# A decoder layer on one core: the first feed-forward product as seven block products (Strassen) in place of eight

## The chip, the core and the metric

The kernel runs on one core of a Trainium2 chip. The metric is the device time of one execution in microseconds; the median of three runs is compared. PE is TensorE (matmuls), DVE is VectorE, ACT is ScalarE, POOL is GpSimd, and SP is the engine whose queue issues all DMAs.

## The reference, cut to what matters

One layer over 512 tokens of width 1024, in float32. The front (norm, a wide input projection, and three token mixers: a state-space scan, differential attention and RWKV-7), the merge of their branches and the output projection stay as they are. What the change works on is the last line but one:

```python
x = x + (merged @ w_out[i]).astype(x.dtype)
h2 = rms_norm(x, norm2_g[i])
gu = h2 @ w_ffn_in[i]                         # 512 x 1024 times 1024 x 5632
x = x + ((silu(gu[..., :D_FF]) * gu[..., D_FF:]) @ w_ffn_out[i]).astype(x.dtype)   # D_FF = 2816
```

## The kernel before

Everything is kept transposed: a tile is 128 channels by the 512 tokens. A dense product (class `Dense`, `__call__`) makes 128 output columns at a time in one PSUM bank and runs over blocks of 128 input channels. To keep float32 precision with float32r matmuls, both factors are split into a high part (a float32r cast, on ACT) and a low part (the remainder, on DVE), and every block takes three matmuls of 512 columns: high x high (L1264), high weights x low activations (L1265), low weights x high activations (L1266). Activations are split once; weights are split as they come: `Dense.load` moves 128x512 values (four blocks, 256 KB) from DRAM (L1201, on SP), casts them (ACT, L1202) and takes the low part (DVE, L1203). Three raw tiles and five each of the high and low parts rotate, and a cast waits until PE is done with the tile that it overwrites.

The code is written in program order; a scheduler decides the order in which each engine gets its instructions, and each engine then works in that order. The stages around the change are these:

- The output projection (`take_res`, eight tiles d): the PSUM result is added to x (DVE, L1475), the sum x2 is multiplied by the norm's gain and split into `act_hi` and `act_lo` (L229, L230), and its squares are added up (`Rms.add`: ACT, L1287; POOL, L1292).
- The first feed-forward product, 22 blocks f: a gate product and an up product, 8 blocks of channels with 3 matmuls each, so 48 matmuls of 512 columns. On the gate's result: times R, the inverse norm (DVE, L1495), tanh (ACT, L1496), L1497 (DVE), and times R again (POOL, L1498, the only instruction that POOL has in a block). Then the product with the up half (DVE, L1501), and the split (L229, L230).
- The second feed-forward product, eight tiles d over 22 blocks (`take_out`): the result is added to x2, which has stayed in SBUF (L1506), and goes out.

## Time and profile before

| | us |
|---|---|
| runs | 1045.37, 1044.82, 1041.97; median 1044.82 |
| profiled execution | 1045.61, its span 1043.8 |
| PE busy | 1007.8 |
| DVE busy | 660.6 |
| ACT busy | 406.1 |
| POOL busy | 136.8 |

The profile records each instruction's start and duration, and what the engine waited for. Matmuls are pipelined: their records overlap, so the distance between starts tells what one costs. On DVE, too, the next instruction starts some 0.08 us before the record of the last one ends. The first feed-forward product runs from about 666 to 917 us of the span.

### The profile page before, as it was taken

How to read it: one execution, taken by the hardware profiler on the slowest of the kernel's cores; microseconds unless marked ns; L12 is line 12 of the kernel's file. 1: busy time of each engine (PE TensorE's matmuls, PEld its weight loads, DVE VectorE, ACT ScalarE, POOL GpSimd, SP SyncE). 2: the span in 40 equal slices, each digit the busy share in tenths (PEclk: the TensorE clock that was granted, in tenths of full speed). 3: DMA queues.
4: the chain of work that ended last, by engine and by line, in shares of the span. 5: the costliest groups of instructions: out<-in, count | busy, mean ns of one | idle time of the engine just before them, and what ended most of it. 6: DMA issues, size and time to landing. Idle time of an engine off the chain costs nothing.

```text
span 1043.8 us, 15814 instructions
## 1 busy us (share of the span) xinstructions
PE 1007.8 (97%) x5664; PEld 808.9 (77%) x5664; DVE 660.6 (63%) x1696; ACT 406.1 (39%) x799; POOL 136.8 (13%) x161
## 2 busy tenths in 40 slices
PE   6999999989899999999999999999999999999998
...
PEclk8999999999999999999999999999999999999999
...
GB/s 233 112 81 99 84 127 52 71 53 42 133 68 77 102 72 131 112 141 92 152 225 261 189 163 99 84 91 94 98 92 91 96 96 91 92 100 110 108 115 41
DMA packets 96798, 114.08 MB, mean 109 GB/s; under 512 B 44400, under 2 KB 46192, under 8 KB 96720
## 3 DMA queue, kind: packets, MB, share of 16 engines
...
q14 instruction: 34, 0.28, 0.1%
...
## 4 chain that ended last, share of the span: by engine, by line
PE 80%; DVE 13%; DMA 3%; issue 2%; ACT 1%; POOL 0%; SPq 0%; DVEq 0%; ACTq 0%; POOLq 0%
PE bank L1265 21%; PE bank L1266 21%; PE bank L1264 21%; DVE wl_s L1203 2%; PE bank L441 1%; PE bank L603 1%; PE bank L1161 1%; PE bank L608 1%; PE bank L1250 1%; PE bank L452 1%; PE bank L1249 1%; PE bank L1248 1%; DMA ar<-ymix 1%; PE bank L235 1%; PE bank L611 1%
## 5 line engine op out<-in xcount | busy, mean ns | idle before, releaser
L1202 ACT CAST wh_s<-wr_s 128x512 fp32r<-128x512 f32 (+1 forms) x286 | 175.1, 614 | 359.8 <-PE bank L1265 323.4
L1264 PE MATMUL bank<-act_hi,wh_s 128*128 128x512 f32 x712 | 288.3, 405 | 6.8 <-ACT wh_s L1202 5.9
L1203 DVE TENSOR_TENSOR wl_s<-wr_s,wh_s 128x512 fp32r<-128x512 f32 (+1 forms) x286 | 200.5, 702 | 144.9 <-ACT wh_s L1202 144.1
L1265 PE MATMUL bank<-act_lo,wh_s 128*128 128x512 f32 x712 | 288.9, 406 | 2.1 <-DVE act_lo L230 2.1
L1266 PE MATMUL bank<-act_hi,wl_s 128*128 128x512 f32 x712 | 288.5, 405 | 0.0
L1264 PEld LDWEIGHTS bank<-act_hi,wh_s 128*128 128x128 f32 x712 | 135.5, 190 | 37.6 <-ACT wh_s L1202 6.1
L1265 PEld LDWEIGHTS bank<-act_lo,wh_s 128*128 128x128 f32 x712 | 135.6, 190 | 33.7 <-DVE act_lo L230 4.3
L1266 PEld LDWEIGHTS bank<-act_hi,wl_s 128*128 128x128 f32 x712 | 135.6, 190 | 29.9 <-issue 0.7
L1265 PE MATMUL bank<-act,wh_s 128*128 128x512 f32 x176 | 69.8, 396 | 0.0
L1264 PE MATMUL bank<-act,wh_s 128*128 128x512 f32 x176 | 69.8, 396 | 0.0
L1266 PE MATMUL bank<-act,wl_s 128*128 128x512 f32 x176 | 69.8, 396 | 0.0
L1265 PE MATMUL bank<-bl,wh_s 128*128 128x512 f32 x112 | 44.7, 399 | 1.4 <-DVE bl L227 1.1
L1264 PE MATMUL bank<-bh,wh_s 128*128 128x512 f32 x112 | 44.6, 398 | 1.0 <-ACT bh L229 0.6
L1266 PE MATMUL bank<-bh,wl_s 128*128 128x512 f32 x112 | 44.4, 396 | 0.0
L1264 PEld LDWEIGHTS bank<-act,wh_s 128*128 128x128 f32 x176 | 33.1, 188 | 8.1
L1266 PEld LDWEIGHTS bank<-act,wl_s 128*128 128x128 f32 x176 | 33.1, 188 | 8.1
L1265 PEld LDWEIGHTS bank<-act,wh_s 128*128 128x128 f32 x176 | 33.1, 188 | 8.1
L1462 POOL TENSOR_TENSOR ar<-ar,ar 128x512 f32<-128x512 f32 x10 | 16.0, 1598 | 176.3 <-DVE ar L1460 176.3
L1498 POOL TENSOR_TENSOR ar<-ar,ar 128x512 f32<-128x512 f32 x15 | 19.8, 1322 | 146.5 <-DVE ar L1497 146.5
L1501 DVE TENSOR_TENSOR ar<-ar,bank 128x512 f32<-128x512 f32 x22 | 15.1, 688 | 37.1 <-PE bank L1266 37.1
L1495 DVE TENSOR_TENSOR ar<-bank,ar 128x512 f32<-128x512 f32 x22 | 15.2, 692 | 36.0 <-PE bank L1266 34.8
L1250 PE MATMUL bank<-wl_s,act_hi 128*128 128x256 f32 x128 | 37.1, 290 | 0.0
...
## 6 DMA issues: line engine op xcount, KB each, us to landing
wr_s<-in_w_in SPq DMA_DIRECT2D x88, 256.0 KB, 2.8
wr_s<-in_w_ffn_in SPq DMA_DIRECT2D x88, 256.0 KB, 2.6
wr_s<-in_w_ffn_out SPq DMA_DIRECT2D x40, 256.0 KB, 2.7
gate<-ar SPq DMA_DIRECT2D x24, 256.0 KB, 2.7
wr_s<-in_w_branch SPq DMA_DIRECT2D x24, 256.0 KB, 3.0
ar<-gate SPq DMA_DIRECT2D x24, 256.0 KB, 3.3
ar<-in_xT SPq DMA_DIRECT2D x16, 256.0 KB, 3.5
wr_s<-in_w_kv SPq DMA_DIRECT2D x16, 256.0 KB, 3.4
```

Source lines behind the costliest of these rows:

```text
L235: self.nc.tensor.matmul(ps[:, b, :], sq[:, b * P:(b + 1) * P], self.c("sel"), start=True, stop=True)
L441: nc.tensor.matmul(pa[:, c * P:(c + 1) * P], kb[rows, 4 * q + c].rearrange("p a t -> p (a t)"), ar[rows, 4 * q + c].rearrange("p a t -> p ...
L1202: nc.scalar.copy(wh, raw)
L1203: nc.vector.tensor_tensor(wl, raw, wh.bitcast(F32), ALU.subtract)
L1250: nc.tensor.matmul(ps, xh, wl[:, j], start=False, stop=k == nk - 1)
L1264: nc.tensor.matmul(ps, wh[:, j], hi(k), start=k == 0, stop=False)
L1265: nc.tensor.matmul(ps, wh[:, j], lo(k), start=False, stop=False)
L1266: nc.tensor.matmul(ps, wl[:, j], hi(k), start=False, stop=k == nk - 1)
L1462: nc.gpsimd.tensor_tensor(g, g, acc, ALU.add)
L1495: nc.vector.tensor_tensor(w, ps, R, ALU.mult)
L1498: nc.gpsimd.tensor_tensor(t, t, R, ALU.mult)
L1501: dense(A["w_ffn_in"][2 * f + 1], KD, h_hi, h_lo, lambda ps: nc.vector.tensor_tensor(t, t, ps, ALU.mult))
```

## The change

The first feed-forward product of a block f is taken as a product of 2x2 blocks: tokens 0 to 255 and 256 to 511, input channels 0 to 511 and 512 to 1023, and the gate and up columns. Strassen's method in Winograd's form makes it from seven products in place of eight, each over 4 blocks of channels, 3 matmuls of 256 columns each: 84 matmuls of 256 columns per block f.

- Activations: `Winograd.take` replaces the split in `take_res`. For d below 4 it makes h, and the difference t1 of its two token halves; for d from 4 on also t2 and t3, three half tiles. All are split into high and low parts; what `act_hi` and `act_lo` hold for d below 4 in the second half of the tokens is t1.
- Weights: `Winograd.pair` loads four raw tiles (a00 and a01 of the gate columns, a10 and a11 of the up columns), now in a ring of six, and makes the sums s1 to s4 on POOL (L1356). Seven tiles are split in place of four: a00, s1, s2, a01, s3, s4, a11.
- Results: products add up in PSUM, and ACT copies a bank's half after four of them (L1381, L1385, L1389, L1395). L1401 and L1403 add copies and PSUM, L1405, L1406 (tanh), L1407 and L1409 (POOL) are the old steps, L1410 (POOL) adds two copies, L1412 and L1413 are the product with the up half, and the split ends the block.
- x2 is written to DRAM in `take_res` and read back in `take_out`, all on SP. Pools that the mixers needed (among them small tiles and constants) are closed after the merge, and their memory is used again; the eight PSUM banks are dealt out anew.

```diff
@@ Env
+    def leave_mixers(self):
+        assert not self.scopes
+        self.mctx.close()
+        self.spool = self.later.enter_context(self.tc.tile_pool(name="fpool", bufs=1, reuse_waits="tile"))
+        self.phase = "f"
+        free = [b for n in ("pd", "prw", "ps") for b in self.pools[n].free]
+        assert len(free) == 8
+        for n, k in (("pf", 4), ("pd", 2), ("ps", 2)):
+            self.pools[n] = Slots(n, [free.pop(0) for _ in range(k)])
...
@@ Dense.load: the raw, high and low weight tiles
-            return E.small(tag, [P, KB * P], dt, bufs=n)[:, 0:w.shape[1] * ncol].rearrange("p (k n) -> p k n", n=ncol)
+            return self.ring(tag, dt, n)[:, 0:w.shape[1] * ncol].rearrange("p (k n) -> p k n", n=ncol)
...
+    def ring(self, tag, dt, n):
+        tiles, at = self.rings.setdefault(tag, ([], [0]))
+        if len(tiles) < n:
+            tiles.append((self.E.spool if self.E.phase else self.E.cpool).tile([P, KB * P], dt, name=self.E.uid(tag)))
+        t = tiles[at[0] % n]
+        at[0] += 1
+        return t
...
+class Winograd:
+    H, N = 4, 256
+    def __init__(self, E, dense, act_hi, act_lo):
+        self.E, self.dense, self.act = E, dense, (act_hi, act_lo)
+        self.t = [E.spool.tile([P, 3, self.H, self.N], F32R, name=f"wg_t{i}") for i in range(2)]
+        self.h = E.arena("wg_h", F32, (P, self.H, T))
+        self.t1 = E.arena("wg_t1", F32, (P, 2 * self.H, self.N))
+        self.banks = E.pools["pf"], E.pools["pd"]
+    def take(self, d, x, gain):
+        E, nc, N = self.E, self.E.nc, self.N
+        V, j = nc.vector, d % self.H
+        hi, lo = self.act
+        a, b = slice(0, N), slice(N, 2 * N)
+        with E.scope("s"):
+            h = self.h[:, d] if d < self.H else E.slot("wg_hd")
+            nc.scalar.activation(h, x, AF.Copy, scale=gain)
+            t1 = self.t1[:, j]
+            if d < self.H:
+                E.split(h[:, a], hi[:, d, a], lo[:, d, a])
+                V.tensor_tensor(t1, h[:, b], h[:, a], ALU.subtract)
+                E.split(t1, hi[:, d, b], lo[:, d, b])
+                return
+            E.split(h, hi[:, d], lo[:, d])
+            t2, t3 = self.t1[:, self.H + j], E.slot("wg_t3")
+            V.tensor_tensor(t2, h[:, b], t1, ALU.subtract)
+            V.tensor_tensor(t3[:, a], h[:, b], self.h[:, j, b], ALU.subtract)
+            V.tensor_tensor(t3[:, b], h[:, a], t2, ALU.subtract)
+            for i, t in enumerate((t2, t3[:, a], t3[:, b])):
+                E.split(t, self.t[0][:, i, j], self.t[1][:, i, j])
+    def pair(self, wg, wu, R, ah, al):
+        E, nc, d = self.E, self.E.nc, self.dense
+        V, G, N, H = nc.vector, nc.gpsimd, self.N, self.H
+        blocks = {}
+        def raw(i, k):
+            t = d.ring("wr", F32, WF)
+            nc.sync.dma_start(t.rearrange("p (k n) -> p k n", n=P), d.blocks((wg, wu)[i], KD, P)[k])
+            return t
+        def add(x, y, op):
+            t = E.slot("wg_s")
+            G.tensor_tensor(t, x, y, op)
+            return t
+        def product(bank, w, b, start):
+            hi, lo = d.ring("wh", F32R, WB[1]), d.ring("wl", F32R, WB[1])
+            E.split(w, hi, lo)
+            ps = bank[:, 0:N]
+            for j in range(H):
+                c = slice(j * P, (j + 1) * P)
+                for n, (x, y) in enumerate(((hi, 0), (hi, 1), (lo, 0))):
+                    nc.tensor.matmul(ps, x[:, c], b(y, j), start=start and j == n == 0, stop=j == H - 1 and n == 2,
+                                     skip_group_check=True)
+        def act(k, t):
+            return lambda y, j: self.act[y][:, H * k + j, t * N:(t + 1) * N]
+        def tee(i):
+            return lambda y, j: self.t[y][:, i, j]
+        x, v = (E._take("pf", (P, 512), False) for _ in range(2))
+        y = E._take("pd", (P, 512), False)
+        keep = E.slot("wg_c", (P, 2, N))
+        keep2 = E.slot("wg_c2", (P, 2, N))
+        a00 = raw(0, 0)
+        product(x, a00, act(0, 0), True)
+        nc.scalar.copy(keep[:, 0], x[:, 0:N])
+        a10, a11 = raw(1, 0), raw(1, 1)
+        s1 = add(a10, a11, ALU.add)
+        product(y, s1, act(0, 1), True)
+        nc.scalar.copy(keep2[:, 1], y[:, 0:N])
+        s2 = add(s1, a00, ALU.subtract)
+        E.free(s1)
+        product(x, s2, tee(0), False)
+        nc.scalar.copy(keep[:, 1], x[:, 0:N])
+        a01 = raw(0, 1)
+        product(v, a01, act(1, 0), True)
+        s3 = add(a00, a10, ALU.subtract)
+        product(x, s3, tee(1), False)
+        E.free(s3)
+        nc.scalar.copy(keep2[:, 0], x[:, 0:N])
+        s4 = add(a01, s2, ALU.subtract)
+        E.free(s2)
+        product(y, s4, act(1, 1), False)
+        E.free(s4)
+        w, t = E.slot("fw"), E.slot("ft")
+        V.tensor_tensor(w[:, 0:N], keep[:, 0], v[:, 0:N], ALU.add)
+        E.free(v)
+        V.tensor_tensor(w[:, N:], keep[:, 1], y[:, 0:N], ALU.add)
+        E.free(y, keep)
+        V.tensor_tensor(w, w, R, ALU.mult)
+        nc.scalar.activation(t, w, AF.Tanh, scale=0.5)
+        V.scalar_tensor_tensor(t, t, 1.0, w, ALU.add, ALU.mult)
+        E.free(w)
+        G.tensor_tensor(t, t, R, ALU.mult)
+        G.tensor_tensor(keep2[:, 1], keep2[:, 0], keep2[:, 1], ALU.add)
+        product(x, a11, tee(2), False)
+        V.tensor_tensor(t[:, N:], t[:, N:], keep2[:, 1], ALU.mult)
+        V.tensor_tensor(t[:, 0:N], t[:, 0:N], x[:, 0:N], ALU.mult)
+        E.free(x, keep2)
+        E.split(t, ah, al, 0.5)
...
@@ trunk_kernel
+    E.leave_mixers()
...
+    win = Winograd(E, dense, act_hi, act_lo)
+    x2dr = [E.dram("x2", [P, T]) for _ in range(KD)]
     def take_res(d):
         def f(ps):
             nc.vector.tensor_tensor(x2[d], x2[d], ps, ALU.add)
-            E.split(x2[d], h_hi(d), h_lo(d), E.pc("n2", d))
+            win.take(d, x2[d], E.pc("n2", d))
             norm.add(x2[d])
+            nc.sync.dma_start(x2dr[d], x2[d])
+            E.free(x2[d])
         return f
...
-            t = E.slot("ft")
-
-            def take_g(ps):
-                w = E.slot("fw")
-                nc.vector.tensor_tensor(w, ps, R, ALU.mult)
-                nc.scalar.activation(t, w, AF.Tanh, scale=0.5)
-                nc.vector.scalar_tensor_tensor(t, t, 1.0, w, ALU.add, ALU.mult)
-                nc.gpsimd.tensor_tensor(t, t, R, ALU.mult)
-
-            dense(A["w_ffn_in"][2 * f], KD, h_hi, h_lo, take_g)
-            dense(A["w_ffn_in"][2 * f + 1], KD, h_hi, h_lo, lambda ps: nc.vector.tensor_tensor(t, t, ps, ALU.mult))
-            E.split(t, ah[f], al[f], 0.5)
+            win.pair(A["w_ffn_in"][2 * f], A["w_ffn_in"][2 * f + 1], R, ah[f], al[f])
     def take_out(d):
         def f(ps):
-            nc.vector.tensor_tensor(x2[d], x2[d], ps, ALU.add)
-            nc.sync.dma_start(outT[d * P:(d + 1) * P], x2[d])
+            with E.scope("s"):
+                x = E.slot("xo")
+                nc.sync.dma_start(x, x2dr[d])
+                nc.vector.tensor_tensor(x, x, ps, ALU.add)
+                nc.sync.dma_start(outT[d * P:(d + 1) * P], x)
```

On DVE, in the middle of the first feed-forward product of the kernel before, one block f reads so (`wl` is the low part of weights, `act` the split result):

```order
L1495 TENSOR_TENSOR ar_13_78<-bank_80,ar_12_77 128x512
L1203 TENSOR_TENSOR wl_s_141<-wr_s_132,wh_s_140 128x512
L1497 SCALAR_TENSOR_TENSOR ar_13_78<-ar_13_78 128x512
L1203 TENSOR_TENSOR wl_s_146<-wr_s_99,wh_s_145 128x512
L1501 TENSOR_TENSOR ar_13_78<-ar_13_78,bank_81 128x512
L1203 TENSOR_TENSOR wl_s_101<-wr_s_111,wh_s_100 128x512
L230 SCALAR_TENSOR_TENSOR act_5964<-ar_13_78,act_5964 128x512
L1203 TENSOR_TENSOR wl_s_113<-wr_s_132,wh_s_112 128x512
```

The same place on DVE in the changed kernel (L244 is the low part, of weights or of sums; L247 that of the result), up to the low part of the block's result; two more L244 follow before the next L1401:

```order
L1401 TENSOR_TENSOR ar_14_82<-ar_13_81,bank_83 128x256
L244 TENSOR_TENSOR wl_144<-ar_13_81,wh_143 128x512
L244 TENSOR_TENSOR wl_149<-ar_14_82,wh_148 128x512
L1403 TENSOR_TENSOR ar_14_82<-ar_13_81,bank_86 128x256
L1405 TENSOR_TENSOR ar_14_82<-ar_14_82,ar_12_80 128x512
L244 TENSOR_TENSOR wl_104<-wr_6080,wh_103 128x512
L1407 SCALAR_TENSOR_TENSOR ar_12_80<-ar_12_80,ar_14_82 128x512
L244 TENSOR_TENSOR wl_116<-ar_12_80,wh_115 128x512
L1412 TENSOR_TENSOR ar_12_80<-ar_12_80,ar_14_82 128x256
L1413 TENSOR_TENSOR ar_12_80<-ar_12_80,bank_84 128x256
L244 TENSOR_TENSOR wl_140<-ar_13_81,wh_137 128x512
L247 SCALAR_TENSOR_TENSOR act_6053<-ar_12_80,act_6053 128x512
```

Eight instructions per block have become fourteen, and the low parts of the next block's weights stand between the steps of this block's result.

On POOL, the end of the output projection and the start of the first feed-forward product in the kernel before:

```order
L1292 TENSOR_TENSOR ar_13_78<-ar_13_78,ar_12_77 128x512 x2
L1292 TENSOR_TENSOR ar_13_78<-ar_13_78 128x512
L1292 TENSOR_TENSOR ar_13_78<-ar_13_78,ar_12_77 128x512
L1498 TENSOR_TENSOR ar_13_78<-ar_13_78,ar_12_77 128x512 x2
L1498 TENSOR_TENSOR ar_12_77<-ar_12_77 128x512
```

POOL in the middle of that product in the changed kernel, between two L1409 (`wr` are raw weights: a00 in 6082, a10 in 102, a11 in 114, a01 in 135; so s3, s1, s2, s4 in this order):

```order
L1409 TENSOR_TENSOR ar_12_80<-ar_12_80 128x512
L1356 TENSOR_TENSOR ar_12_80<-wr_6082,wr_102 128x512
L1356 TENSOR_TENSOR ar_12_80<-wr_102,wr_114 128x512
L1356 TENSOR_TENSOR ar_13_81<-ar_12_80,wr_6082 128x512
L1356 TENSOR_TENSOR ar_14_82<-wr_135,ar_13_81 128x512
L1410 TENSOR_TENSOR ar_13_81<-ar_13_81 128x256
L1409 TENSOR_TENSOR ar_13_81<-ar_13_81,ar_12_80 128x512
```

One instruction per block has become six: the four sums for the next block, then L1410 and L1409 of this one.

## Rows read from the trace of the kernel before

**Rows 1.** Page: busy time per engine; tenths busy per slice; chain that ended last.

```profile
PE 1007.8 (97%) x5664; PEld 808.9 (77%) x5664; DVE 660.6 (63%) x1696; ACT 406.1 (39%) x799; POOL 136.8 (13%) x161
...
PE   6999999989899999999999999999999999999998
...
PEclk8999999999999999999999999999999999999999
...
PE 80%; DVE 13%; DMA 3%; issue 2%; ACT 1%; POOL 0%; SPq 0%; DVEq 0%; ACTq 0%; POOLq 0%
```

**Rows 2.** Busy us by stretch: length, PE, PEld, DVE, ACT, POOL, clock, DMA.

```profile
750.00:800.00 50.00, 50.00 (x215) 40.21 (x214) 23.71 (x36) 16.89 (x27) 5.17 (x4) 1.00 0.31 95
```

**Rows 3.** Timeline, POOL, first feed-forward product: start, duration, instruction [idle before, releaser].

```profile
699.37 1.30 POOL L1498 TENSOR_TENSOR ar<-ar 128x512 f32<-128x512 f32 x1 [9.83 <-DVE ar L1497]
...
913.03 1.29 POOL L1498 TENSOR_TENSOR ar<-ar,ar 128x512 f32<-128x512 f32 x1 [9.94 <-DVE ar L1497]
```

**Rows 4.** Timeline, PE, a key and value product: first and last of 34 matmuls.

```profile
317.09 0.28 PE L1248 MATMUL bank<-wh_s,act_hi 128*128 128x256 f32 x1
...
321.04 0.28 PE L1248 MATMUL bank<-wh_s,act_hi 128*128 128x256 f32 x1
```

**Rows 5.** Groups by line and shape: count, busy us, mean ns, idle before.

```profile
L1202 ACT CAST wh_s<-wr_s 128x512 fp32r<-128x512 f32 x278 | 171.9, 620 | 354.3 <-PE bank L1265 317.9 <-issue 15.3 <-DMA wr_s<-in_w_in 6.1
...
L229 ACT ACTIVATE act<-ar 128x512 fp32r<-128x512 f32 x22 | 13.9, 633 | 7.9 <-DVE ar L1501 7.9
...
L1089 ACT ACTIVATE ar<-bank 128x256 f32<-128x256 f32 x8 | 3.1, 384 | 5.9 <-PE bank L1250 4.4 <-DVE ar L1152 1.5
...
L1203 DVE TENSOR_TENSOR wl_s<-wr_s,wh_s 128x512 fp32r<-128x512 f32 x278 | 197.1, 710 | 142.7 <-ACT wh_s L1202 141.8 <-issue 0.2
...
L1203 DVE TENSOR_TENSOR wl_s<-wr_s,wh_s 128x256 fp32r<-128x256 f32 x8 | 3.4, 424 | 2.2 <-ACT wh_s L1202 2.2
```

**Rows 6.** POOL's L1498 and L1462 (ns min/median/max); timeline around one L1462.

```profile
L1498 POOL TENSOR_TENSOR ar<-ar,ar x15: 1286/1296/1707, 678.1 to 913.0; 128x512 f32<-128x512 f32 x15
...
L1462 POOL TENSOR_TENSOR ar<-ar,ar x10: 1298/1608/1675, 558.9 to 621.9; 128x512 f32<-128x512 f32 x10
...
579.51 0.68 DVE L1203 TENSOR_TENSOR wl_s<-wr_s,wh_s 128x512 fp32r<-128x512 f32 x1
579.77 1.58 POOL L1462 TENSOR_TENSOR ar<-ar 128x512 f32<-128x512 f32 x1 [1.23 <-DVE ar L1460]
```

**Rows 7.** POOL's L916 (ns); timeline of DVE and POOL around the longest.

```profile
L916 POOL TENSOR_TENSOR ar<-s_pr,ar x4: 1493/1592/4812, 102.4 to 263.6; 128x512 f32<-128x512 f32 x4
...
263.56 4.81 POOL L916 TENSOR_TENSOR ar<-s_pr,ar 128x512 f32<-128x512 f32 x1 [6.27 <-PE bank L978]
...
264.68 0.67 DVE L683 TENSOR_TENSOR ar<-s_rr,ar 128x512 f32<-128x512 f32 x1
...
265.28 0.15 DVE L219 SCALAR_TENSOR_TENSOR rqy_rw<-rqt_rw,rqi_rw 128x8 f32<-128x8 f32 x1
...
267.32 1.08 DVE L219 SCALAR_TENSOR_TENSOR rqy_rw<-rqt_rw,rqy_rw 128x8 f32<-128x8 f32 x1
```

**Rows 8.** Timeline, DVE and POOL around another sum of POOL.

```profile
218.08 0.18 DVE L685 TENSOR_TENSOR ar<-ar,ar 128x8 f32<-128x8 f32 x1
...
222.94 1.29 POOL L918 TENSOR_TENSOR ar<-ar,ar 128x512 f32<-128x512 f32 x1
222.99 1.26 DVE L685 TENSOR_TENSOR ar<-ar,ar 128x16 f32<-128x16 f32 x1
```

**Rows 9.** Timeline, DVE and POOL: an instruction of DVE that reads PSUM.

```profile
271.36 0.67 DVE L307 TENSOR_TENSOR ar<-bank,R 128x512 f32<-128x512 f32 x1
271.37 1.09 POOL L917 TENSOR_TENSOR ar<-s_pi,ar 128x512 f32<-128x512 f32 x1
```

**Rows 10.** Page, DMA issues: count, KB each, median us from issue to landing.

```profile
wr_s<-in_w_ffn_in SPq DMA_DIRECT2D x88, 256.0 KB, 2.6
...
ymix<-ar SPq DMA_DIRECT2D x12, 256.0 KB, 2.2
```

65 lines of the change are left out of this document (36 added, 29 removed).

## The prediction

> **What bounds the kernel now.** The page comes first: PE, the engine of the matmuls, is busy for 97% of the span, and 80% of the chain that ended last is PE's, most of it in the three matmul lines of the dense product [rows 1]. The next view is the table by stretches. The change works in the first feed-forward product, from about 666 to 917 us, and in a stretch from its middle PE is busy for all of 50 us at full clock, while DVE (VectorE) is busy for 24, ACT (ScalarE) for 17 and POOL (GpSimd) for 5 [rows 2]. So PE alone sets the time there, and the change starts from there. Its unit is one block f of 22: 128 gate and 128 up columns. POOL has exactly one instruction per block, L1498, so its start times give the period. From the first to the last of the 20 that one answer lists there are 19 periods: (913.03 - 699.37)/19 = 11.245 us [rows 3]. A block has 2 x 8 x 3 = 48 matmuls of 512 columns, so one costs 0.234 us. The durations in the rows (0.39 us) overlap; the spacing of starts is the price.
>
> **PE's part.** A block becomes 7 x 4 x 3 = 84 matmuls of 256 columns. The trace has such matmuls in the key and value products: 34 in a row start from 317.09 to 321.04 us, so 33 steps of 0.120 us [rows 4], barely more than half of 0.234. PE's need falls from 11.25 to 84 x 0.1197 = 10.05 us per block, by 1.19 us, or 26 us over 22 blocks. That is all that the arithmetic can give, and only if everything else fits into 10.05 us.
>
> **What the other engines get, each alone** [rows 5]. ACT now has seven casts of 0.62 us, four copies of 256 columns out of PSUM (the nearest row, L1089, has 0.385), the tanh and the split at 0.63: 7.15 us. DVE has ten instructions of 512 columns (seven low parts, the product with R at L1405, L1407 and the low part of the result) and four of 256 (L1401 to L1413 are lines of the changed kernel, as in the orders shown with the change). The low part's row says 0.71 us, but back to back the next one starts after 0.60 us, as 264.68 to 265.28 shows [rows 7]; the 256-wide low part is 0.28 us shorter (0.424 against about 0.70), so 0.32. DVE's sum is 10 x 0.60 + 4 x 0.32 = 7.3 us. POOL had one instruction per block and gets six: four sums of weights, L1409, and L1410 at half width. Undisturbed, one of 512 columns takes 1.295 us; I take 0.65 for the half: 7.1 us. Each alone would fit. The question is whether they run side by side.
>
> **DVE and POOL do not.** In the stage before, L1462, a POOL sum with the same operands, has a median of 1.608 us against 1.296 for L1498 [rows 6]. Its timeline tells why. DVE's L1203 starts at 579.51 and would let the next go after 0.60 us, at 580.11; the POOL instruction starts at 579.77 and ends at 581.35, that is 1.24 us after DVE lets go, so it did next to nothing during the 0.34 us of overlap [rows 6]. The extreme is another sum [rows 7]: L916 (median of its four 1.592 us) takes 4.81 us while DVE runs instructions end to end, many with two SBUF inputs as at 264.68, and at 267.32 an instruction of 128x8 that otherwise takes 0.15 us holds DVE for 1.08 us, while POOL at last works. It goes the other way round as well [rows 8]: a 128x16 DVE instruction that starts at 222.99, just behind a POOL sum, takes 1.26 us. About 0.18 of that is its own (the row of 128x8 on the same line), so POOL kept it out for 1.08 us; with the 0.05 us between the starts a POOL sum occupies what they share for 1.13 us. An instruction with one input in PSUM is not held: L307 takes 0.67 us beside L917 [rows 9].
>
> The Trainium skill has this as a rule, in "SBUF — State Buffer", section "SBUF: two separate sides": one port pair serves GpSimd and the VectorE instructions that have two SBUF inputs or run in a two-port mode, it is locked for a whole instruction, and the other engine waits. The trace agrees, except that POOL's hold is shorter than its record (1.13 of 1.295 us). By the rule, with every record held whole, a block would take 14.5 us and the kernel 1119, the time of rival (b) below; by the holds that the rows show it takes 13.0.
>
> **The sum for a block.** Of DVE's fourteen instructions eleven have two SBUF inputs: ten of 0.60 and L1412, of 0.32 us: 6.3. L1401, L1403 and L1413 read PSUM and are free. POOL: 5 x 1.13, and for the half width between 0.4 and 0.65, so 0.55: 6.2. Together 12.5 us that can't overlap, against 10.05 on PE. To this come gaps: DVE finishes L1405, ACT does the tanh (0.63 us), DVE can fill it with one low part of 0.60, then L1407, then POOL's L1409, then L1412, and all of these sit on the shared resource in this order. I walked one period through the two orders shown with the change, letting a ready DVE instruction go ahead of POOL as in [rows 7]. L1409 ends at 0; L1412 goes first, POOL's first sum follows until 1.5; four DVE instructions run end to end until 3.9, and POOL's second sum until 5.0 and third until 6.3; one low part until 6.9, POOL's fourth sum until 8.0; a low part until 8.6, L1410 until 9.2; L1405 and a low part until 10.35; L1407 at 10.5, a low part until 11.8, and the next L1409 ends at 13.0. PE is never late in it: its products start as their low parts come, and each block leaves PE about 3 us idle. So 13.0 us per block. ACT's casts, the ring of five weight tiles and the loads (1 MB per block, 2.6 us from issue to landing [rows 10], six buffers) have slack at that pace.
>
> First product: 22 x (13.0 - 11.245) = +38.6 us.
>
> **The rest.** Eight times in the output projection DVE and ACT also make the half sums of h: for the last four tiles DVE has four instructions of 512 columns (the residual, the low part of h, two low parts of weights) and six of 256, and POOL adds up the squares. That is 4 x 0.60 + 6 x 0.32 + 1.13 = 5.5 us against 24 x 0.234 = 5.6 us of PE: covered, with nothing to spare. After PE's last projection matmul, the chain to the last half sum (residual, scale, square, high part, half sum and its parts) is about 4 to 4.5 us, and products 0, 1 and three quarters of 2 cover 2 x 1.44 + 1.08 = 3.96 us. I add 1 us, and 0.5 us for the hand-over to the second feed-forward product. Parking x2: eight writes queue on SP among the weight loads. Each waits for the residual of its tile; nine of the sixteen projection loads stand ahead of the first write and one to three between two, so the loads run two tiles ahead of the write that they queue behind. The eight reads come during the last product. A write of this size lands after 2.2 us [rows 10]: nothing. The memory reuse puts three early loads into the merge of the branches, with no wait but that of the DMA itself. The first 530 us are issued in a slightly different order on every engine; there PE has small gaps that can open or close, so 0, with 4 us either way.
>
> Against the profiled execution, 1045.6 us: 1045.6 + 38.6 + 1.5 = 1085.7, say **1086**. The median of the three runs is 0.8 us lower than that execution; I don't correct for it.
>
> **Rivals.** (a) Faster: DVE and POOL share so little in this stage that PE binds. For it: in this stage of before only one of L1498's rows is long (1.707 us, [rows 6]), and each engine alone would fit. It needs POOL to occupy the shared resource for no more than (10.05 - 6.3)/5.5 = 0.68 us per sum, against 1.08 at the least [rows 8]. Then a block is 10.05 us plus perhaps 0.3 where a product waits for ACT to copy the bank that it adds to: 22 x (10.3 - 11.245) = -21, so 1026. 14%. Between it and the forecast, where some sums hide, lie 1040 to 1062: 4%.
> (b) Slower still: POOL is starved, as for 4.81 us in [rows 7], the sums of weights come late, and then ACT, DVE and PE wait for them in turn; DVE and POOL run one after the other over their full records: 10 x 0.70 + 0.40 + 5 x 1.295 + 0.65 = 14.5 us, and 22 x (14.5 - 11.245) + 1.5 = +73, so 1119; as a case 1104 to 1130. It decides as soon as DVE, behind a late sum, has nothing else ready; the end-to-end group L247 and two low parts is where that starts. 16%.
> (c) The change does not do what it says, because half-width matmuls cost more than half: priced, at 0.120 against 0.117 it takes 0.2 us per block and decides nothing here. A lower clock through PE's idle time: the page's first slice, with PE at 6 tenths, still has 8 tenths of the clock [rows 1], and PE has 3 us per block to give.
>
> **How the numbers follow.** The forecast, 66%, spans blocks of 12.2 us (POOL at 1.08 us, hardly a gap) to 13.8: 1062 to 1104 with the 4 us of the front. The range leaves out (a), half of the case between and the end of (b), together just under 20%: 1050 to 1122. Faster by over 0.3%: 0.14; within 0.3%, about what a measurement of this kernel can tell from no change: 0.02; slower by more: 0.84.
>
> **What would show it.** Right: in the first product PE's busy share falls to about 80%, the 256-column matmuls wait for low parts of DVE, POOL's sums have medians well above 1.3 us, and DVE and POOL together fill the stretch. Wrong: POOL's sums at 1.3 us beside a DVE that starts every 0.60 us, and PE full; then (a) holds. If POOL rows of 3 us and more stand beside an idle DVE, (b).

## The result, and the profile after

The changed kernel takes 1101.44 us (median of four runs, 1098.74 to 1106.69) beside 1044.92 for the kernel before: a ratio of 1.055, 95% interval 1.051 to 1.060. The prediction was 1086, in a range of 1050 to 1122. Its profiled execution took 1098.74 us, with a span of 1096.1, which is 52.3 us more than before.

The page of the changed kernel, busy time of each engine:

```profile
PE 1002.2 (91%) x6456; PEld 852.6 (78%) x6456; DVE 822.8 (75%) x1860; ACT 472.3 (43%) x977; POOL 306.8 (28%) x271
```

[rows 1] had PE at 97%, DVE at 63% and POOL at 13%. The table by stretches, for 150 us from the middle of the first product (columns as in [rows 2]):

```profile
750.00:900.00 150.00, 120.00 (x918) 115.41 (x916) 132.66 (x154) 67.48 (x141) 93.03 (x66) 0.95 0.24 78
```

PE is busy for 80% of it, where [rows 2] had 100%, and its granted clock is 0.95 instead of 1.00. DVE and POOL together show 225.7 us of records in 150 us: they do not work side by side for all that time, because a record runs on while its instruction waits for the other engine.

Where the 52.3 us came from is read from first and last starts. The changed kernel, timeline by line: L1626 (residual behind the output projection), L1405 (gate times R) in its two forms, L1651 (last addition of the second product):

```profile
L1626 DVE TENSOR_TENSOR ar<-ar,bank x8: 673/686/689, 623.1 to 667.3; 128x512 f32<-128x512 f32 x8
...
L1405 DVE TENSOR_TENSOR ar<-ar,ar x17: 692/694/1276, 682.6 to 971.8; 128x512 f32<-128x512 f32 x17
L1405 DVE TENSOR_TENSOR ar<-ar x5: 691/692/693, 726.7 to 947.3; 128x512 f32<-128x512 f32 x5
...
L1651 DVE TENSOR_TENSOR ar<-ar,bank x8: 686/687/689, 987.8 to 1092.5; 128x512 f32<-128x512 f32 x8
```

The same three places in the kernel before:

```profile
L1475 DVE TENSOR_TENSOR ar<-ar,bank x8: 686/689/690, 626.7 to 666.1; 128x512 f32<-128x512 f32 x8
...
L1495 DVE TENSOR_TENSOR ar<-bank,ar x22: 691/692/692, 675.9 to 910.9; 128x512 f32<-128x512 f32 x22
...
L1506 DVE TENSOR_TENSOR ar<-ar,bank x8: 686/688/690, 932.0 to 1040.2; 128x512 f32<-128x512 f32 x8
```

- Up to the first residual: 623.1 - 626.7 = -3.6 us.
- A block: (971.8 - 682.6)/21 = 13.77 us, before (910.9 - 675.9)/21 = 11.19. That is +2.58 us, and +56.8 over 22 blocks.
- The second product: seven tiles take 104.7 us instead of 108.2, so -0.5 us for each of eight, -4.0.
- The transition from the projection and to the second product is what remains: from the first residual to the first output tile the changed kernel needs 364.7 us, before 305.3; 59.4 - 56.8 + 0.5 = +3.1 us.

### One block, row by row

DVE in the changed kernel, from one L1412 to the next (start, duration, instruction; in brackets the idle time before it):

```profile
813.74 1.51 DVE L1412 TENSOR_TENSOR ar<-ar 128x256 f32<-128x256 f32 x1 [1.18 <-POOL ar L1409]
815.17 0.41 DVE L1413 TENSOR_TENSOR ar<-ar,bank 128x256 f32<-128x256 f32 x1
815.50 0.68 DVE L244 TENSOR_TENSOR wl<-ar,wh 128x512 fp32r<-128x512 f32 x1
816.34 0.69 DVE L247 SCALAR_TENSOR_TENSOR act<-ar,act 128x512 fp32r<-128x512 f32 x1 [0.15 <-ACT act L246]
817.11 3.51 DVE L244 TENSOR_TENSOR wl<-wr,wh 128x512 fp32r<-128x512 f32 x2
820.55 0.41 DVE L1401 TENSOR_TENSOR ar<-ar,bank 128x256 f32<-128x256 f32 x1
820.88 2.59 DVE L244 TENSOR_TENSOR wl<-ar,wh 128x512 fp32r<-128x512 f32 x2
...
825.23 0.69 DVE L1407 SCALAR_TENSOR_TENSOR ar<-ar,ar 128x512 f32<-128x512 f32 x1
825.84 0.69 DVE L244 TENSOR_TENSOR wl<-ar,wh 128x512 fp32r<-128x512 f32 x1
827.70 1.50 DVE L1412 TENSOR_TENSOR ar<-ar,ar 128x256 f32<-128x256 f32 x1 [1.18 <-POOL ar L1409]
```

POOL in the same block, its five instructions of 512 columns and L1410:

```profile
812.04 1.67 POOL L1409 TENSOR_TENSOR ar<-ar,ar 128x512 f32<-128x512 f32 x1 [3.08 <-DVE ar L1407]
813.67 1.29 POOL L1356 TENSOR_TENSOR ar<-wr,wr 128x512 f32<-128x512 f32 x1
817.11 1.27 POOL L1356 TENSOR_TENSOR ar<-wr,wr 128x512 f32<-128x512 f32 x1 [2.14 <-DVE act L247]
818.46 1.62 POOL L1356 TENSOR_TENSOR ar<-ar,wr 128x512 f32<-128x512 f32 x1
820.16 1.62 POOL L1356 TENSOR_TENSOR ar<-wr,ar 128x512 f32<-128x512 f32 x1
821.73 1.19 POOL L1410 TENSOR_TENSOR ar<-ar 128x256 f32<-128x256 f32 x1
```

From L1412 to L1412 it is 13.96 us. DVE's own work is the prediction's 7.3 us (ten at 0.60, four at 0.32). It is kept out by POOL for 1.51 - 0.41 = 1.10 us in L1412, 3.51 - 1.28 = 2.23 in the two low parts at 817.11 (1.28 is what two take undisturbed), and 2.59 - 1.28 = 1.31 in the two at 820.88: 4.64 us. It has nothing to do for 1.18 us while POOL's L1409 runs, and the rest, 0.8, are small gaps. So DVE uses half of the block for its own work, and POOL has taken or holds up most of the other half.

Not every block is like this one. Of the 19 inner blocks, from the end of one L1409 to the next, 13 take 13.92 to 13.96 us. In the other six (13.44 to 13.46 us), DVE goes first where the second sum and two low parts start at once (817.11 above), and POOL waits:

```profile
845.00 2.39 DVE L244 TENSOR_TENSOR wl<-wr,wh 128x512 fp32r<-128x512 f32 x2
...
850.69 0.41 DVE L1403 TENSOR_TENSOR ar<-ar,bank 128x256 f32<-128x256 f32 x1
...
845.00 1.84 POOL L1356 TENSOR_TENSOR ar<-wr,wr 128x512 f32<-128x512 f32 x1 [2.14 <-DVE act L247]
...
850.18 1.18 POOL L1410 TENSOR_TENSOR ar<-ar 128x256 f32<-128x256 f32 x1
```

Here L1403, which reads PSUM and is not held, stands beside L1410. In the block above it starts at 823.39, after L1410 has ended (822.92), and takes 0.45 us of its own. So who goes first at this one place is worth 0.5 us. PE's granted clock is not what makes the longer blocks: it is 0.87 in the block of 13.45 us that holds these rows and 1.00 in the block of 13.96 us above.

The groups of the page say the same over all blocks (the last numbers are the mean of one in ns, and the idle time before them); a low part had 710 ns in [rows 5], and L1498 a median of 1296 in [rows 6]:

```profile
L1366 PE MATMUL bank<-wg_t,wh 128*128 128x256 f32 x528 | 110.1, 307 | 49.3 <-ACT ar L1389 41.8
...
L244 DVE TENSOR_TENSOR wl<-ar,wh 128x512 fp32r<-128x512 f32 x88 | 92.7, 1067 | 2.9 <-ACT wh L243 2.0
...
L244 DVE TENSOR_TENSOR wl<-wr,wh 128x512 fp32r<-128x512 f32 x66 | 79.1, 1221 | 2.4 <-ACT wh L243 0.5
...
L1356 POOL TENSOR_TENSOR ar<-wr,wr 128x512 f32<-128x512 f32 x44 | 60.8, 1382 | 47.5 <-DVE act L247 43.4
```

PE's waits have another name. The waits of the changed kernel from 700 to 960 us (total us, times, longest):

```profile
ACT act L246 <- DVE ar L1413: 58.2, 19, 3.1
...
POOL ar L1356 <- DVE act L247: 40.7, 19, 2.1
PE bank L1366 <- ACT ar L1389: 40.6, 19, 2.3
...
DVE ar L1412 <- POOL ar L1409: 22.5, 19, 1.2
```

PE waits for L1389, a copy that ACT must make before the next product adds to the bank. The copy is late because it stands on ACT behind L246, and L246 waits for L1413, which stands on DVE behind the held L1412. The wait that the page names at PE is the far end of a chain that begins with DVE and POOL.

### The profile page after: what moved, and what is told of

It reads as the page before. It is cut to its first block, busy times and chain, and to the rows that moved or that the text cites. A ratio compares the mean times of both kernels' runs of the same rounds, so it can differ in the third digit from the quotient of the medians.

```text
span 1096.1 us, 17987 instructions
## 1 busy us (share of the span) xinstructions
PE 1002.2 (91%) x6456; PEld 852.6 (78%) x6456; DVE 822.8 (75%) x1860; ACT 472.3 (43%) x977; POOL 306.8 (28%) x271
## 5 line engine op out<-in xcount | busy, mean ns | idle before, releaser
L1220 ACT CAST wh<-wr 128x512 fp32r<-128x512 f32 x198 | 120.7, 612 | 224.2 <-PE bank L1292 185.4
L1221 DVE TENSOR_TENSOR wl<-wr,wh 128x512 fp32r<-128x512 f32 x198 | 136.9, 694 | 83.5 <-ACT wh L1220 82.8
L1291 PE MATMUL bank<-act_hi,wh 128*128 128x512 f32 x360 | 149.4, 415 | 9.1 <-ACT wh L1220 5.8
L1366 PE MATMUL bank<-wg_t,wh 128*128 128x256 f32 x528 | 110.1, 307 | 49.3 <-ACT ar L1389 41.8
L1292 PE MATMUL bank<-act_lo,wh 128*128 128x512 f32 x360 | 148.8, 413 | 1.3 <-DVE act_lo L247 1.3
L1293 PE MATMUL bank<-act_hi,wl 128*128 128x512 f32 x360 | 148.0, 411 | 0.0
L1366 PE MATMUL bank<-act_hi,wh 128*128 128x256 f32 x352 | 104.9, 298 | 0.9 <-ACT wh L243 0.9
L244 DVE TENSOR_TENSOR wl<-ar,wh 128x512 fp32r<-128x512 f32 x88 | 92.7, 1067 | 2.9 <-ACT wh L243 2.0
L1291 PEld LDWEIGHTS bank<-act_hi,wh 128*128 128x128 f32 x360 | 69.5, 193 | 23.8 <-ACT wh L1220 5.8
L1292 PEld LDWEIGHTS bank<-act_lo,wh 128*128 128x128 f32 x360 | 69.2, 192 | 16.2 <-DVE act_lo L247 3.0
L244 DVE TENSOR_TENSOR wl<-wr,wh 128x512 fp32r<-128x512 f32 x66 | 79.1, 1221 | 2.4 <-ACT wh L243 0.5
L1293 PEld LDWEIGHTS bank<-act_hi,wl 128*128 128x128 f32 x360 | 69.2, 192 | 13.5 <-issue 0.2
L1366 PEld LDWEIGHTS bank<-act_hi,wl 128*128 128x128 f32 x352 | 73.1, 208 | 3.2 <-DVE wl L244 3.2
L1366 PEld LDWEIGHTS bank<-act_hi,wh 128*128 128x128 f32 x352 | 73.4, 209 | 1.2 <-ACT wh L243 1.1
L1356 POOL TENSOR_TENSOR ar<-wr,wr 128x512 f32<-128x512 f32 x44 | 60.8, 1382 | 47.5 <-DVE act L247 43.4
L1366 PEld LDWEIGHTS bank<-act_lo,wh 128*128 128x128 f32 x352 | 73.3, 208 | 0.0
```

The source lines that it names most:

```text
L244: nc.vector.tensor_tensor(lo, src, hi.bitcast(F32), ALU.subtract)
L1220: nc.scalar.copy(wh, raw)
L1221: nc.vector.tensor_tensor(wl, raw, wh.bitcast(F32), ALU.subtract)
L1291: nc.tensor.matmul(ps, wh[:, j], hi(k), start=k == 0, stop=False)
L1292: nc.tensor.matmul(ps, wh[:, j], lo(k), start=False, stop=False)
L1293: nc.tensor.matmul(ps, wl[:, j], hi(k), start=False, stop=k == nk - 1)
```

## Experiments

Theory A is the prediction's: DVE's instructions with two SBUF inputs and POOL's sums can't run side by side, and that sets the block. The rivals: B, the sums simply come late on the chain to the products; C, DVE alone is full; and later D, the slots in which the sums lie close a loop. In the table a block is the distance from the first to the last of 22 instructions that come once a block, over 21; the busy times are those of 750 to 900 us of the span. PE's grow where its granted clock is lower: with L1412 and L1413 exchanged it shows 128.4 us for 924 matmuls at 0.87, in the changed kernel 120.0 for 918 at 0.95.

| kernel | us | ratio to before, 95% | block, us | PE | DVE | POOL |
|---|---|---|---|---|---|---|
| before | 1044.92 | | 11.19 | 150.0 | 71.1 | 16.8 |
| changed | 1101.44 | 1.055 (1.051 to 1.060) | 13.77 | 120.0 | 132.7 | 93.0 |
| sums unread | 1093.56 | one run | 13.36 | 122.7 | 133.2 | 101.2 |
| no sums | 1028.38 | one run | 10.50 | 142.2 | 113.4 | 37.1 |
| sums on DVE | 1050.12 | 1.0065 (1.0041 to 1.009) | 11.44 | 131.1 | 137.5 | 40.2 |
| all on DVE | 1036.61 | 0.9923 (0.9901 to 0.9945) | 10.68 | 145.5 | 149.8 | 0.0 |
| L1412, L1413 exchanged | 1097.27 | 1.049 (1.046 to 1.052) | 13.60 | 128.4 | 132.9 | 94.1 |
| slots of their own | 1103.65 | 1.056 (1.054 to 1.058) | 13.61 | 120.8 | 122.4 | 90.6 |
| L1409 on DVE | 1079.54 | one run | 12.86 | 123.4 | 129.2 | 84.6 |
| both of these | 1072.66 | one run | 12.43 | 126.5 | 138.8 | 82.8 |
| R at the end, all on DVE | 1022.45 | 0.9772 (0.9744 to 0.9799) | 10.08 | 149.5 | 148.8 | 0.0 |

### The hand-over of the sums, or their making

Edit (the other three products likewise take a00, a01 and a11):

```diff
-        product(y, s1, act(0, 1), True)
+        product(y, a10, act(0, 1), True)
```

> The changed kernel with its four sums of weights still made on POOL, but read by nobody: the products that took s1 to s4 take raw tiles of the weights (the output is therefore not the reference's). POOL and DVE have all the instructions that they had; only the hand-over of the sums is gone. Theory A (DVE and POOL can't work side by side, and the sum of their holds sets the block): the holds are still 6.3 us of DVE and 6.2 of POOL, so a block can't be below 12.5 us, and is 12.5 to 13.6 instead of 13.8; 1070 to 1094 us. Theory B (a sum comes late, and the chain sum, split, product, copy of the bank, next product sets the block; the engines themselves have room): with the sums off the chain a block falls to PE's 10.05 to 10.6 us, 1016 to 1028 us.

And with the four `add` lines gone:

> The same products from raw tiles, and the four sums left out altogether (part of the computation is missing). POOL keeps L1409 and L1410. A: the holds fall to 6.3 + 1.13 + 0.55 = 8.0 us, below PE's 10.05; a block is 10.05 to 10.6 us and the kernel 1016 to 1028. B: the same. Theory C (DVE alone is full in these blocks, 44 of 50 us by the page): DVE has what it had, the block stays near 13.8 and the kernel near 1099 us.

Measured: 13.36 us per block with sums that nobody reads, 10.50 without them (1028.38 us, 0.4 above the range of the expectation). Of the 3.27 us between the changed kernel and the one without sums, 0.41 belong to waiting for a sum and 2.86 to its being made at all. B is out, and C too: DVE falls to 113 of 150 us when POOL makes no sums, though its own work in a block is the same. In the kernel with unread sums POOL adds while DVE is in the middle of its low parts:

```profile
804.99 3.15 DVE L244 TENSOR_TENSOR wl<-wr,wh 128x512 fp32r<-128x512 f32 x2
...
805.97 1.63 POOL L1356 TENSOR_TENSOR ar<-wr,ar 128x512 f32<-128x512 f32 x1
807.55 1.75 POOL L1356 TENSOR_TENSOR ar<-wr,wr 128x512 f32<-128x512 f32 x1
```

Two low parts take 3.15 us, undisturbed 1.28, beside two sums that nobody waits for.

### The sums on the other engine

```diff
         def add(x, y, op):
             t = E.slot("wg_s")
-            G.tensor_tensor(t, x, y, op)
+            V.tensor_tensor(t, x, y, op)
```

> The four sums of weights are made by DVE instead of POOL; nothing else is changed. A: a sum now holds the shared resource for DVE's 0.60 us instead of POOL's 1.13: 6.3 + 4 x 0.60 + 1.0 for the three instructions that read PSUM = 9.7 us on DVE, and POOL's 1.7 beside it, 11.4 us, with gaps up to 12.2; 1046 to 1063 us. C: DVE, already full, gets 2.4 us more: a block of 16.2 us, 1150 us. B: a sum stands in DVE's queue behind whatever is there, so it comes no earlier than before: 13.5 to 14 us, 1092 to 1103.

> The four sums, L1409 and L1410 all on DVE; POOL has nothing to do in the first product. A: 7.3 + 5 x 0.60 + 0.32 = 10.6 us of DVE per block with nobody to wait for; 10.6 to 11.3 us, 1028 to 1044 us, so at or a little below the kernel before (11.245 us per block). C: slower than with the four sums alone on DVE, over 1150 us. B: 1092 us or more, as with the four sums alone.

Measured: 11.44 and 10.68 us per block. The engine that shows the most records gets 2.4 us more work, and the block becomes 2.3 us shorter; with all of POOL's work it becomes 3.1 us shorter. C expected the opposite. The middle of the first product in these two kernels, first with the sums alone on DVE, then with everything on DVE:

```profile
750.00:900.00 150.00, 131.14 (x1088) 128.59 (x1087) 137.52 (x234) 84.38 (x169) 40.19 (x26) 0.99 0.29 91
```

```profile
750.00:900.00 150.00, 145.47 (x1174) 138.83 (x1173) 149.84 (x280) 89.74 (x182) 0.00 (x0) 1.00 0.31 97
```

In the second, DVE does 280 instructions where the changed kernel's DVE did 154 in the same time, with no idle time: 10.68 us against 10.6 for the sum of its starts' distances. Here DVE's own work is the bound. The kernel is a little faster than the one before.

### What holds L1412

```diff
-        V.tensor_tensor(t[:, N:], t[:, N:], keep2[:, 1], ALU.mult)
         V.tensor_tensor(t[:, 0:N], t[:, 0:N], x[:, 0:N], ALU.mult)
+        V.tensor_tensor(t[:, N:], t[:, N:], keep2[:, 1], ALU.mult)
```

> The changed kernel with L1412 and L1413 exchanged: the product of the half whose up value still lies in PSUM goes first, the one that needs L1410's result second. In the trace of the changed kernel DVE's L1412 takes 1.51 us (0.41 undisturbed) because POOL's third sum starts just ahead of it, and L1413 (0.4 us) waits behind it. A (the hold of that sum keeps L1412 out): the instruction that reads PSUM is not held and runs during the hold, the other then follows; 0.3 to 0.4 us per block off the chain, 13.4 to 13.5 instead of 13.8, 1090 to 1094 us, and the second of the two still takes about 1.1 us. Rival (the 1.51 us are the wake-up behind POOL's L1409, not the hold): the first of the two now takes 1.5 us whichever it is, the block stays at 13.8, 1098 to 1102 us.

In this kernel the first of the two reads PSUM:

```profile
815.54 0.42 DVE L1412 TENSOR_TENSOR ar<-ar,bank 128x256 f32<-128x256 f32 x1 [1.18 <-POOL ar L1409]
815.88 1.18 DVE L1413 TENSOR_TENSOR ar<-ar 128x256 f32<-128x256 f32 x1
...
815.47 1.30 POOL L1356 TENSOR_TENSOR ar<-wr,wr 128x512 f32<-128x512 f32 x1
```

Beside the same sum it takes 0.42 us at once, and the one with two SBUF inputs is held. So it is the hold, not the waking up, and an input in PSUM escapes it, as [rows 9] had it. The gain was smaller than expected: a block of 13.60 instead of 13.4 to 13.5, and the confidence intervals of the two ratios overlap, so that the time alone would not settle it. The mean of the changed kernel mixes two kinds of block. Here POOL's second sum goes first in every inner block, and against the 13.94 us of such blocks the exchange gives 0.34 us, as expected.

### The price of a hold

The dense product of before, in the memory layout of after (see "The rest of the change"), with eight sums per block added on POOL (the ring of raw weights also has six tiles instead of three; the rest of the edit is left out here):

```diff
...
         nc.vector.tensor_tensor(wl, raw, wh.bitcast(F32), ALU.subtract)
+        for i in range(self.more):      # 2 in the first product, else 0
+            nc.gpsimd.tensor_tensor(self.spare[i % 2], raw, raw, ALU.add)
```

> The same kernel with eight more sums per block on POOL, two behind the low part of each piece of weights of the dense first product; nobody reads them, and six buffers of raw weights instead of three keep POOL's reading from holding up loads. PE needs 11.25 us per block as before. A: the holds are 6 x 0.60 of DVE (four low parts, the product with 1 + tanh, the last low part; the two that read PSUM are free) and 9 x 1.13 of POOL, 13.8 us, so a block of 13.8 to 14.4 us and 1100 to 1114 us, though DVE and POOL have no result to hand each other that they had not before. POOL alone (no sharing): 9 x 1.295 = 11.65 us, 1050 to 1057 us. B (only a sum that is waited for costs): 1041 to 1049.

Measured: 1057.77 us (one run; the same without the sums 1037.91). A's 1100 us is wrong, by far. In the middle of the product the block is 11.93 us (818.09 - 806.16, two starts of L1654), and over the whole product 11.6. DVE in this kernel, and POOL over the same time:

```profile
808.91 1.52 DVE L247 SCALAR_TENSOR_TENSOR act<-ar,act 128x512 fp32r<-128x512 f32 x1
810.36 1.53 DVE L1221 TENSOR_TENSOR wl<-wr,wh 128x512 fp32r<-128x512 f32 x1
811.81 0.68 DVE L1651 TENSOR_TENSOR ar<-bank,ar 128x512 f32<-128x512 f32 x1
...
807.40 6.83 POOL L1223 TENSOR_TENSOR spare_sf<-wr 128x512 f32<-128x512 f32 x5
```

The exclusion is as plain as can be: 1.52 us for what takes 0.69, next to 0.68 for L1651, which reads PSUM. But where both engines have work queued, one instruction of each fits into 1.45 us (808.91, 810.36, 811.81), not into the 1.13 + 0.60 = 1.73 that the prediction adds up. So in this queue of sums each holds the shared resource for 1.45 - 0.60 = 0.85 us. That the rest of the 1.13 us is a start that lies beside a DVE instruction when POOL is already waiting is a guess that no row shows. POOL loses little (9 instructions in 11.93 us, 1.33 each, against starts 1.24 us apart when it is undisturbed: 807.40 - 806.16), and DVE loses 0.8 to 0.9 us for each instruction that meets a sum. Here DVE has the time to lose (its records fill 111.6 of 150 us), so nobody notices; POOL is full (150.0 of 150) and sets the time. The expectation's case "POOL alone" gave 1050 to 1057.

The 0.85 us do not hold in the changed kernel. There, too, four POOL instructions follow each other within 0.1 us (817.11 to 822.92), but the two low parts beside the first two take 820.55 - 817.11 = 3.44 us, 1.72 for a low part and a sum. One difference is that the added sums read nothing that POOL made, while s2 reads s1 and s4 reads s2. Whether that is the reason is not tested.

### Slots, and POOL's place in the chain

With holds of 0.85 us, DVE's 6.3 us and POOL's five and a half instructions are 11.0 us, well below 13.77. What makes the rest? First the slot for which the sum at 817.11 waits 2.14 us:

```diff
-            t = E.slot("wg_s")
+            t = E.small("wg_s", [P, T], bufs=3)
...
-        E.free(s1)
...
```

> The changed kernel, in which the four sums of weights get three tiles of their own instead of slots from the pool that t, w and the copies share. Nothing else is edited; POOL still makes all sums, L1409 and L1410. In the changed kernel the first sum of a block takes the slot that L247, the last step of the block before, gives back, and waits 2.14 us for it; that closes a loop: first sum, second, fourth, its product, L1403, L1405, L1406, L1407, L1409, L1412, L1413, L246, L247, first sum. A (the holds themselves set the block, at 1.13 us for a POOL sum): 12.5 us is a floor, a block of 12.5 to 13.4, 1070 to 1092 us. D (this loop sets the block; the holds only stretch what lies in it, and a POOL sum that alternates with DVE costs less than 1.13 us, as the eight unread sums beside the dense product show): without the slot's wait of 2.14 us a block takes 11.0 to 12.2 us, 1038 to 1064 us.

13.61 us per block and no faster in all (1103.65, of which some 6 us lie ahead of the first residual, at 629.1 instead of 623.1 us), outside the ranges of both A and D. The mean hides that neighbouring blocks differ. From one L1401 to the next it is 11.65 us at 814.33, with a granted clock of 1.00, and then 15.95:

```profile
825.98:841.93 15.95, 12.45 (x85) 12.26 (x85) 12.20 (x15) 6.27 (x14) 11.10 (x9) 0.79 0.26 81
```

In the long one the clock is 0.79, and DVE waits 1.14 us for a cast and 1.24 us for PE's bank. So slots of their own bring nothing here, but this run can't show by itself that the loop has no part, because the edit changes more than the slots: with the slots gone, the scheduler put the first sum ahead of L1409 and the second right behind it, and L1408 (the old L1412) is held for 1.48 us as before. Then the other way into the loop:

```diff
-        G.tensor_tensor(t, t, R, ALU.mult)
+        V.tensor_tensor(t, t, R, ALU.mult)
```

> The changed kernel with L1409 alone on DVE: it no longer passes from DVE to POOL and back, and no sum of POOL starts in front of L1412. A: the holds fall by 1.13 and rise by 0.60, 12.0 us, a block of 12.0 to 12.4, 1059 to 1068 us. D: the loop loses 1.67 + 0.15 us of POOL's L1409 with its two hand-overs, gets 0.60 on DVE, and loses 1.1 us of L1412: 13.8 - 2.3 = 11.5 us, 1045 to 1055 us.

12.86 us, between the changed kernel and both expectations. And both edits together:

> The two last edits together: L1409 on DVE, and three tiles of their own for the four sums. With L1409 alone on DVE a block took 12.86 us; there POOL waited 2.6 us twice per block for a slot that L244 or L247 gives back, and DVE 1.5 us for the cast of a late sum. Tiles of their own alone brought nothing (13.9 us). D in its weaker form (the slots bind as soon as POOL is out of the chain of the activations): DVE's 1.5 us of idling go, 11.3 to 11.8 us, 1041 to 1055 us. A with a hold of 0.85 us, as the unread sums beside the dense product show it: 6.3 + 0.6 + 4 x 0.85 + 0.45 = 10.75 us is the floor, and the same range or less. If DVE loses about 1 us to each sum whatever the order is: 7.9 us of its own and 4 to 4.6 us of waiting, 11.9 to 12.5 us, 1055 to 1072 us. If nothing binds but the exclusion at 1.13 us: 12.0 to 12.9, 1057 to 1081.

12.43 us, 1072.66 in all. (The 13.9 us in this expectation for the slots alone was read from single blocks; the mean over 21 is 13.61.) D's weaker form, and the holds of 0.85 us as the only bound, expected under 11.8; both are out. In most blocks DVE has next to no idle time left, as here, 0.29 us between one L1401 and the next (810.81 and 822.98; the lines are numbered a little lower in this kernel). Its held instructions in that stretch:

```profile
810.81 1.32 DVE L1401 TENSOR_TENSOR ar<-ar,ar 128x512 f32<-128x512 f32 x1
...
814.65 1.80 DVE L244 TENSOR_TENSOR wl<-wg_s_sf,wh 128x512 fp32r<-128x512 f32 x1
...
817.04 1.47 DVE L244 TENSOR_TENSOR wl<-wr,wh 128x512 fp32r<-128x512 f32 x1
...
820.94 1.68 DVE L244 TENSOR_TENSOR wl<-wg_s_sf,wh 128x512 fp32r<-128x512 f32 x1 [0.29 <-ACT wh L243]
```

0.63 + 1.12 + 0.79 + 1.00 = 3.5 us of holds, 7.9 of its own work, 0.3 idle, and 0.4 in small gaps: 12.2 us in this stretch. Six of the 21 blocks are different: their granted clock is 0.87, DVE waits 0.3 to 1.5 us for a cast and 0.4 to 0.7 us for PE's bank, and they take 13.0 to 13.3 us; one more, near the start, takes 15.17 us at 0.78. What part of that is the clock's is not shown.

The expectation's third and fourth cases both have the mean block in their range; the time is 0.7 us above the third's and inside the fourth's. This run does not tell them apart. The unread sums beside the dense product rule out 1.13 us as a price that holds everywhere, and the changed kernel, with its four POOL instructions in a row, rules out that a row is always cheaper. The theory that stands at the end is A: the bound is DVE's queue, its own work plus up to 1.1 us for each POOL instruction that it meets (0.5 for L1410), plus the time in which it waits for POOL's L1409. How the scheduler would have to order POOL for the 1.45 us pairs is not tried.

### The rest of the change

The changed kernel with the dense first product of before, and then also without the traffic of x2:

```diff
...
-            win.pair(A["w_ffn_in"][2 * f], A["w_ffn_in"][2 * f + 1], R, ah[f], al[f])
...
+            dense(A["w_ffn_in"][2 * f], KD, h_hi, h_lo, take_g)      # as before
+            dense(A["w_ffn_in"][2 * f + 1], KD, h_hi, h_lo, lambda ps: nc.vector.tensor_tensor(t, t, ps, ALU.mult))
...
```

> All the rest of the change with the dense first product of the kernel before: x2 goes to DRAM and comes back, the memory of the mixers is reused, and gate and up are eight block products of 512 columns. If the rest of the change costs nothing, as the sum has it (half sums of h are not made here): 1041 to 1049 us. If the writes or reads of x2 stand in the way of loads, or the other order of the first 530 us does harm: over 1050.

> The kernel with the dense first product and the rest of the change, but x2 stays on the chip: no writes to DRAM and no reads; the memory of the mixers is still reused, so the ring of weights and the later tiles lie where they lie in the changed kernel. With parking it took 1037.9 us, 8 less than the kernel before, and its second product ran at 0.227 us per matmul of 512 columns instead of 0.234. If parking gives that (x2 no longer in the way): 1044 to 1047 us and 0.234. If the new places of the tiles do: 1036 to 1040 us and 0.227.

Measured: 1037.91 us, ratio 0.9927 (0.9899 to 0.9955), and 1040.81, ratio 0.9955 (0.9934 to 0.9975). Both are faster than the kernel before, and their intervals overlap: parking costs nothing that can be seen, and what is gained without it, 4 us, comes with the rest of the change (new places of the tiles, the ring of weights, the PSUM banks; not told apart). The first is faster than expected (1041 to 1049), the second 0.8 us above the range for the new places, though its 0.227 us per matmul are that case's. 50 us of the second product, in the kernel before, with x2 parked, and with x2 on the chip:

```profile
960.00:1010.00 50.00, 50.00 (x215) 40.18 (x214) 14.87 (x24) 11.78 (x20) 0.00 (x0) 1.00 0.36 106
```

```profile
960.00:1010.00 50.00, 50.00 (x222) 41.42 (x221) 14.56 (x23) 11.83 (x20) 0.00 (x0) 1.00 0.38 113
```

```profile
960.00:1010.00 50.00, 50.00 (x222) 41.40 (x221) 14.83 (x24) 11.29 (x21) 0.00 (x0) 1.00 0.42 124
```

222 matmuls instead of 215 at the same granted clock: 0.227 us each (104.7 us for 7 tiles of 66) instead of 0.234.

### A version that beats both

With everything on DVE, DVE was the bound by 0.6 us. One of its steps is not needed in each block: the second factor R belongs to a token, so it can be applied to the result of the second product.

```diff
-        V.tensor_tensor(t, t, R, ALU.mult)          # in each of 22 blocks
...
-                nc.vector.tensor_tensor(x, x, ps, ALU.add)
+                y = E.slot("xp")
+                nc.vector.tensor_tensor(y, ps, R, ALU.mult)      # in each of eight tiles
+                nc.vector.tensor_tensor(x, x, y, ALU.add)
```

> The kernel with the four sums, L1409 and L1410 all on DVE, where DVE has no idle time left in the first product (49.9 of 50 us, 10.68 us per block), with L1409 taken out: the second factor R belongs to a token, so it is applied once to each tile of the second product (eight more DVE instructions there, which read PSUM) instead of to each of 22 blocks. A: DVE's sum falls by 0.6 us to 10.1, PE's 10.05 is met, a block of 10.2 to 10.5 us; 1025 to 1034 us, 4 to 10 us less than with L1409 on DVE. If another wait (a copy of a bank by ACT) sets the block by now: as with L1409 on DVE, 1034 to 1038.

Measured: 1022.45 us, ratio 0.977 (0.974 to 0.980), better than expected. The middle of its first product:

```profile
750.00:900.00 150.00, 149.54 (x1242) 146.19 (x1241) 148.79 (x281) 94.67 (x194) 0.00 (x0) 1.00 0.35 112
```

PE is full again, and a block takes 10.08 us: 84 x 0.120, the whole saving that the method has to give in a block. Not all of the 23.7 us to the kernel before (1046.18 us beside these runs) are Strassen's: the same kernel with the dense product took 1037.91 us, so 8.3 come with the rest of the change and 15.5 with the seven products. A block saves 11.15 - 10.08 = 1.07 us against that kernel, but the two transitions, from the first residual to the first block's L1405 (there L1647) and from the last to the first output tile, take 60.4 + 16.1 us instead of 47.8 + 20.6, 8.1 more.

## Why the prediction was right, and by which step it was off

- **PE's part**, 84 x 0.1197 = 10.05 us: right. With R at the end PE is full at 10.08 us a block, so a half-width matmul costs barely more than half (0.120 us beside 11.15/48 = 0.232), and rival (c) decides nothing, as was said. The lower clock that it names did come (0.95 from 750 to 900 us), but the blocks at 0.87 are not the longer ones.
- **DVE and POOL exclude each other**: right, and the cause of the loss (2.86 of 3.27 us a block belong to the making of the sums). Rival (a), PE as the bound, needed a hold under 0.68 us; it is 0.85 at the least. What escapes, an input in PSUM, was right too. The rule named from the Trainium skill ("SBUF — State Buffer", section "SBUF: two separate sides") agrees in who excludes whom; with the lock kept for the whole of an instruction, counted from start to start, a pair would take 1.24 + 0.60 = 1.84 us, and the trace shows 1.72 in the changed kernel and 1.45 beside the dense product.
- **The hold of 1.13 us**: right for this kernel. L1412, starting 0.07 us after a sum, is through 1.58 us after the sum's start, of which 0.41 its own, so 1.17. The two low parts at 817.11 lose 3.44 - 1.20 = 2.24 us to two sums, and the stretch of the next two, L1401 included, is 823.39 - 820.55 - 1.20 = 1.64 us longer than their own time, with a sum and L1410 beside it, where the prediction has 1.13 + 0.55. It is no general price: for the unread sums beside the dense product it gave 1100 us, measured 1058.
- **The sum of 12.5 us**: right. In the block from 813.74 the eleven DVE instructions with two SBUF inputs are 6.33 us, and POOL's share is 1.10 + 2.24 + 1.64, and 1.26 for L1409 (827.70 - 825.84 - 0.60), together 6.24 instead of 6.2: 12.57 us.
- **The walk from there to 13.0 us per block**: the step that was off; measured 13.77, and 13.96 in this block. It gave no time to the three DVE instructions that "read PSUM and are free". They are free only where they stand beside a POOL instruction. L1401 does; L1413 comes behind the held L1412 when the sum is over, and takes 0.33 us, and L1403 comes when L1410 is over, and takes 0.45. The waits around ACT's steps and small gaps make another 0.59 (0.24 + 0.17 + 0.18 at 815.50, 816.34 and 824.45); the walk had 0.5 in all.
- **"A ready DVE instruction goes ahead of POOL"**, taken from [rows 7], where DVE ran without a gap: wrong at L1412 in every inner block, where DVE has just waited for L1409 and POOL has its next sum at hand. That costs little by itself, since sum and L1412 are both through 1.54 us after the end of L1409, and the walk had 1.5; but it puts L1413 behind the hold, and the exchange of the two gave 0.34 us back. At 817.11 it was wrong in 13 of 19 blocks, and there it is worth 0.5 us, because L1403 then misses L1410.
- **22 blocks**: +56.8 us instead of +38.6. Of the 18.2 us between them 17.0 are the block, 13.77 instead of 13.0, and 1.2 the kernel before, whose blocks are 11.19 us over all 22 and 11.245 without the first two.
- **PE waits for low parts**: wrong in the name. PE waits for ACT's copy L1389, behind an ACT instruction that waits for DVE. The walk had no queue for ACT, and called ACT's casts slack.
- **The rest, +1.5 us**: the transitions cost 3.1 (1.5 predicted), the front gave 3.6 (within the 4 that were left open), the second product gave 4.0. The memory reuse, priced at nothing, was the missed term: with the front it takes 7.6 us off an error of 18.2 in the walk and 1.6 in the transitions, which is why the span came out only 12.2 us above the forecast. So a part of the nearness is luck, the front's above all: in the changed kernel and the variants of it the first residual starts anywhere from 622.5 to 629.1 us. Parking x2 cost nothing, as predicted. The bounds of the forecast are added up wrongly by 2 to 3 us: blocks of 12.2 to 13.8 us with 4 us either way give 1064 to 1107 by its own sum, not 1062 to 1104.
- **Rival (b)** described POOL as the one that starves. It was the other way round: POOL's sums kept means of 1.38 to 1.61 us, the longest 1.85, and DVE's low parts went from 0.71 to 1.07 and 1.22.
- **What would show it**: PE at 80%, and DVE and POOL filling the stretch, came as written; sums "well above 1.3 us" only for the two that follow another sum (1.62 in the block shown, the other two 1.27 and 1.29), since most of the waiting is in DVE's records.
